# A two-layer decoder trunk: other places for modulation sums, a vector moved to the second mixing, and rotary tables on GpSimd

## The chip, the cores and the metric

The kernel runs on 1 core of a Trainium2 chip. The metric is the device time of one execution in microseconds (us). The profile names five engines: PE (matrix products), DVE (VectorE), ACT (ScalarE), POOL (GpSimd) and SP (here only a queue of DMA transfers). Each executes its own instructions in a fixed order and waits where an input is not ready.

## The reference, cut to what matters

One sequence of 256 tokens with 1024 features passes two layers, in float32. Each layer has three sub-layers: a SwiGLU feed-forward (inner width 2816), a token mixing, and a second feed-forward. Each sub-layer normalises its input and changes it by a shift, a scale and a gate that come from a vector `c`:

```python
cos, sin = rope_tables(positions, ATT_HEAD_DIM // ROPE_FRACTION)
c_act = jax.nn.silu(c)
for l in range(DEPTH):
    mod = c_act @ ada_w[l] + ada_b[l]            # 1024 x 9216
    sh1, sc1, g1, sh2, sc2, g2, sh3, sc3, g3 = jnp.split(mod, N_MOD, axis=-1)
    h = modulate(rms_norm(x, norm_ffn1[l]), sh1, sc1)
    x = x + 0.5 * g1[:, None, :] * swiglu(h, ffn1_w_in[l], ffn1_w_out[l])
    h = modulate(rms_norm(x, norm_mix[l]), sh2, sc2)
    x = x + g2[:, None, :] * token_mix(h, cos, sin, mix_w_in[l], sgu_w[l], sgu_b[l], mix_w_out[l])
    h = modulate(rms_norm(x, norm_ffn2[l]), sh3, sc3)
    x = x + 0.5 * g3[:, None, :] * swiglu(h, ffn2_w_in[l], ffn2_w_out[l])
return rms_norm(x, final_norm)
```

`modulate(h, shift, scale)` is `h * (1 + scale) + shift`. `swiglu` is `(silu(g) * u) @ w_out` with `g, u` the two halves of `h @ w_in`. `token_mix` runs a causal gating and an attention over selected keys side by side; its queries and keys are rotated by the `cos` and `sin` tables, which are computed once from the positions.

## The kernel before, in words

**Weights.** Every matrix is streamed once, in units of 512 KB. SP's queue loads a unit into one of seven raw buffers (`dma_fill`, L328; the DMAs are issued in L350 to L364). A product in full precision is made of three products of rounded parts (`mm3`, L514; L694 for both token blocks at once): high by high, high by low, low by high. So each raw unit is split before PE may use it: ACT writes the high part `whi` (L474), then DVE writes the low part `wlo` (L479), into a ring of ten pairs (`NB`). A raw buffer is free when `wlo` has been written.

**Modulation.** A vector of 1024 values takes eight more units of 512 KB, out of `ada_w`, through the same seven raw buffers and the same queue. ACT multiplies the first by a column of `c` (L454), DVE adds the other seven (L459), into `aacc`. Then the 128 partitions are still to be summed. For a shift (kind B) or a scale (kind A) `col_finish` (L397) does it with two times four PE transposes (L780) and two DVE reductions (L405). For a gate (kind G) `aacc` is itself split by L474 and L479 and multiplied by ones on PE (L374, L375; `ada_finish`, L368), and DVE adds the bias (L376). Either sum is put off by `ADA_D` = 8 work items (`defer`): it comes into the engines' queues eight items after the last of the vector's blocks.

**Six phases.** One to three are the first layer's feed-forward, mixing and feed-forward; four to six the second layer's. A feed-forward has 66 weight units: 44 of `w_in` and 22 of `w_out`. The units of `w_in` come in chunks of eight (one of four). From the second chunk on (`joint_chunk`, L686) both blocks of 128 tokens are multiplied together, 24 matmuls of 256 columns a unit. At a chunk's end ACT does silu out of PSUM (L716), DVE the product (L717), ACT and DVE the split (L511, L512). These four wait for PE to finish the chunk, and what stands behind them in the queues of ACT and DVE waits with them. Then `project` (L602) multiplies by `w_out`: block 0 runs seven units ahead of block 1 (`LAG`), half a unit's work each; afterwards the blocks take turns.

**The order of the stream.** `weave` (L256) puts modulation blocks evenly between weight units; `FA0`, `FA1` (phase one) and `F0`, `F1` (phases three to six) bound the stretch of units, `MA0`, `MA1` that of the mixings. `VA1`, `VA2`, `VA3`, `VB1`, `VB2` say how many vectors belong to each phase: before, these are five, one, four, five, none, and the rest (one) in the last. They are taken in turn from one list in the order of need (A, B, G of sub-layer one, then two, then three; the very first A and B are made at the start).

**How far splits run ahead.** `pump` (L427) emits splits and modulation blocks after each item. It stops where `lead` split weights lie ahead of PE (L444). `joint_gen` (L731) yields how many units of its chunk are left, and L1292 makes of it `min(8, 4 + left)`: toward the end of a chunk the lead shrinks from 8 to 5, but in the last chunk it stays 8 (`left` is 0 there).

**Rotary tables.** `rope_tables` (L154) is a generator; phase one takes two of its steps after each joint unit. Before, DVE does all of it (eight memsets, products, casts to integer and back, range reduction), and ACT the sines (L189 to L199).

Of the kernel before, what the change touches and what calls it, by code (L numbers as in the profile page):

```python
# [13 lines left out]
ALU = mybir.AluOpType  # L14
# [14 lines left out]
TAIL = 3  # L29
VX = 188  # L30
ADA_D = 8
D_EVP = 0
D_V = 0
D_V2 = 0
# [14 lines left out]
RED_ACT = 1  # L49
SCOL = 3  # L50
SPUMP = 0
FA0 = 20
FA1 = 62
NSRAW = 8
NV = 2
GAP = 0
VA1 = 5
VA2 = 1
VA3 = 4
VB1 = 5  # L60
VB2 = 0
F0 = 14
F1 = 62
ADA0_ACT = 1
# [31 lines left out]
PI_IN = 3.1415925  # L96
# [3 lines left out]
def trunk(ctx, tc, x_in, c_in, pos_in, ada_w, ada_b, norm_ffn1, ffn1_w_in, ffn1_w_out,  # L100
# [53 lines left out]
    def rope_tables():  # L154
        posf = small.tile([P, 2], F32, name="posf", tag="posf")
        V.tensor_copy(posf, posi)
        yield
        invt = small.tile([P, 8], F32, name="invt", tag="invt")
        for i, f in enumerate(INV_FREQ):
            V.memset(invt[:, i:i + 1], f)  # L160
            yield
        for b in range(2):
            V.tensor_scalar(ang[:, b, :], invt, posf[:, b:b + 1], None, op0=ALU.mult)
            yield
        nf = const.tile([P, 2, 8], F32, name="nf")
        ni = const.tile([P, 2, 8], I32, name="ni")
        t2 = const.tile([P, 2, 8], F32, name="t2")
        for m in (2048.0, 1.0):
            V.tensor_scalar(nf, ang, 1.0 / (2 * math.pi * m), None, op0=ALU.mult)
            yield  # L170
            V.tensor_copy(ni, nf)
            yield
            V.tensor_copy(nf, ni)
            yield
            for cc in (C1, C2, C3):
                V.scalar_tensor_tensor(ang, nf, -cc * m, ang, op0=ALU.mult, op1=ALU.add)
                yield
        V.tensor_scalar(nf, ang, math.pi, None, op0=ALU.is_gt)
        yield
        V.tensor_scalar(t2, ang, -math.pi, None, op0=ALU.is_lt)  # L180
        yield
        V.tensor_tensor(nf, nf, t2, op=ALU.subtract)
        yield
        for cc in (C1, C2, C3):
            V.scalar_tensor_tensor(ang, nf, -cc, ang, op0=ALU.mult, op1=ALU.add)
            yield
        V.tensor_scalar(ang, ang, PI_IN, -PI_IN, op0=ALU.min, op1=ALU.max)
        yield
        S.activation(sinT[:, :, 8:16], ang, AF.Sin)  # L189
        yield  # L190
        S.activation(sinT[:, :, 0:8], ang, AF.Sin, scale=-1.0)
        yield
        V.scalar_tensor_tensor(t2, ang, -1.0, ang, op0=ALU.mult, op1=ALU.max)
        yield
        V.tensor_scalar(t2, t2, -1.0, math.pi / 2, op0=ALU.mult, op1=ALU.add)
        yield
        S.activation(cosT[:, :, 0:8], t2, AF.Sin)
        yield
        S.activation(cosT[:, :, 8:16], t2, AF.Sin)  # L199
        yield  # L200
# [80 lines left out]
    for l in range(DEPTH):  # L281
        u1, chunks = ffn_units(ffn1_w_in[l], ffn1_w_out[l])
        u2 = mix_units(mix_w_in[l], mix_w_out[l])
        u3, _ = ffn_units(ffn2_w_in[l], ffn2_w_out[l])
        n_f = KD + KF
        phases += [("f", l, 1, n_f if l else KF), ("m", l, 2, len(u2)), ("f", l, 3, n_f)]
        vl = []
        for q in range(3):
            vl.append(sum((vecs(a, [nm]) for a, nm in names[:cuts[3 * l + q]]), []))
            names = names[cuts[3 * l + q]:]  # L290
        w1 = weave(u1, vl[0], FA0 if l == 0 else F0, FA1 if l == 0 else F1)
        if l == 0:
            w0 = []
            for g in range(NG):
                w0 += [dict(k="s", g=g, j0=j0) for j0 in (list(range(0, KD, SJ)) if g else
                                                     list(range(SJ, KD, SJ)) + [0])]
                w0 += [w1[2 * g], w1[2 * g + 1], w1[KD + g]]
            w1 = w0 + w1[KD + NG:]
        seq += w1
        seq += weave(u2, vl[1], MA0, MA1)  # L300
        seq += weave(u3, vl[2], F0, F1)
# [125 lines left out]
    def pump(quota=2, force=False, now=False, hi_only=False):  # L427
# [5 lines left out]
        while sp[0] < len(seq) and quota > 0:  # L433
# [15 lines left out]
            if e["k"] == "a":  # L449
                j = e["j"]  # L450
                if j == 0:
                    aacc = accs[0] = aap.tile([P, D], F32, name="aacc", tag="aacc")
                    if ADA0_ACT:
                        S.activation(aacc, e["raw"], AF.Copy, scale=ccol[:, 0:1])  # L454
                    else:
                        V.tensor_scalar(aacc, e["raw"], ccol[:, 0:1], None, op0=ALU.mult)
                else:
                    aacc = accs[0]
                    V.scalar_tensor_tensor(aacc, e["raw"], ccol[:, j:j + 1], aacc,  # L459
                                           op0=ALU.mult, op1=ALU.add)  # L460
                if j == KD - 1 and e["kind"] != "G":
                    defer(ADA_D, col_finish(e, aacc))
            if need:
                ring.append(False)
                hi = hlp.tile([P, D], F32R, name="whi", tag="whi")
# [265 lines left out]
    def joint_gen(env, first):  # L731
        for ch in range(first, len(chunks)):
            left = 8 if chunks[ch][1] == 512 else 4
            for _ in joint_chunk(env, ch):
                left -= 1
                yield left if ch + 1 < len(chunks) else 0


    def rope(t, nh, b, pool):
# [594 lines left out]
```

## Time and profile before

| what | before |
|---|---|
| time of three runs | 1011.24, 1011.47, 1011.87 us; median 1011.47 us |
| profiled execution | 1015.82 us, of which the profiled span is 1014.1 us |
| PE / DVE / ACT / POOL busy | 97% / 77% / 53% / 3% of the span |
| moved by DMA | 253.41 MB, 250 GB/s over the span |
| phase one's products by `w_out` begin | near 152.7 us |
| first, second mixing (from one norm's statistics to the next) | 220.08 to 326.77 us, 710.75 to 813.68 us |

The share of busy time is a mean over the phases. A matmul's start is exact and its end modelled, so PE's true pace is read from start to start. "PEclk" in the windows is the granted clock: 1.00 is the upper of two levels (2.4 GHz), 0.5 the lower (1.2 GHz), and numbers between are means over a stretch.

### The profile page before, as it was taken

To read this page: it belongs to the slowest core of one execution; us is meant where nothing else is said; L and a number is where in the kernel's file an instruction comes from. 1 tells how busy PE (TensorE), PEld (TensorE's weight loads), DVE (VectorE), ACT (ScalarE), POOL (GpSimd) and SP (SyncE) were. 2 spreads that over 40 slices of the span, in tenths; PEclk is the share of its full clock that TensorE was granted. 3 is DMA by queue.
4 is the path that set the end of the run, shared out by engine and by line. 5 is a ranking of instruction groups with operands and counts; after the bars stand their busy time and mean duration, and the time that the engine had idled before them with its cause. 6 is when DMAs were issued, how large, how long until landed. Compare 5 with 4: busy or idle time off the path is not lost.

```text
span 1014.1 us, 16715 instructions
## 1 busy us (share of the span) xinstructions
PE 986.3 (97%) x6468; PEld 881.0 (87%) x6468; DVE 777.9 (77%) x1088; ACT 536.3 (53%) x804; POOL 26.4 (3%) x39
## 2 busy tenths in 40 slices
PE   7999997999999999999999999999999999999997
PEld 6899995887787899998888999878778889999886
DVE  6888988777897877789678688895878785576554
ACT  6465454356577744545455454543657765454341
POOL 4000000000000000000000000000000000000000
PEclk9999998999999999999999999989999999999999
DMA  9988899956655577889858779987554556576731
GB/s 333 380 286 321 316 352 353 356 181 225 188 189 157 169 270 280 300 314 356 289 162 315 276 291 344 358 328 235 167 152 138 166 158 207 169 252 243 262 115 42
DMA packets 110031, 253.41 MB, mean 250 GB/s; under 512 B 8754, under 2 KB 27236, under 8 KB 109952
## 3 DMA queue, kind: packets, MB, share of 16 engines
q1 hardware_dynamic: 109120, 251.20, 70.8%
q8 instruction: 50, 0.82, 0.3%
q0 software_dynamic: 544, 0.63, 0.3%
q10 hardware_dynamic: 288, 0.52, 0.1%
q14 instruction: 29, 0.24, 0.1%
HBM read 251.27 MB, written 1.05 MB: 249 GB/s over the span
## 4 chain that ended last, share of the span: by engine, by line
PE 73%; DVE 12%; DMA 7%; ACT 5%; issue 3%; POOL 0%; SPq 0%; POOLq 0%; ACTq 0%; DVEq 0%
PE bank L694 28%; PE bank L515 14%; PE bank L517 13%; PE bank L516 13%; DVE wlo L479 3%; DVE aacc L459 3%; PE bank L780 2%; DMA raw<-in_ffn_w_in_dram 2%; DMA raw<-in_ffn_w_out_dram 2%; DMA sraw<-in_ada_w_dram 2%; ACT whi L474 2%; DVE xm L717 1%; ACT aThi L511 1%; DMA raw<-in_ada_w_dram 1%; DVE aacc L1101 1%
## 5 line engine op out<-in xcount | busy, mean ns | idle before, releaser
L474 ACT ACTIVATE whi<-raw 128x1024 fp32r<-128x1024 f32 (+1 forms) x328 | 334.9, 1046 | 233.1 <-PE bank L517 126.6
L479 DVE TENSOR_TENSOR wlo<-raw,whi 128x1024 fp32r<-128x1024 f32 (+1 forms) x313 | 373.9, 1212 | 91.7 <-ACT whi L474 89.7
L694 PE MATMUL bank<-hThi,whi 128*128 128x256 f32 x1216 | 336.1, 280 | 1.6 <-ACT hThi L1139 1.6
L694 PE MATMUL bank<-hThi,wlo 128*128 128x256 f32 x1216 | 333.2, 277 | 0.0
L694 PE MATMUL bank<-hTlo,whi 128*128 128x256 f32 x1216 | 323.7, 277 | 0.0
L694 PEld LDWEIGHTS bank<-hThi,whi 128*128 128x128 f32 x1216 | 228.3, 188 | 2.9 <-ACT hThi L1139 2.0
L694 PEld LDWEIGHTS bank<-hThi,wlo 128*128 128x128 f32 x1216 | 229.1, 188 | 0.7 <-issue 0.7
L694 PEld LDWEIGHTS bank<-hTlo,whi 128*128 128x128 f32 x1216 | 222.6, 188 | 0.3
L515 PE MATMUL bank<-whi,aThi 128*128 128x512 f32 (+1 forms) x374 | 144.1, 385 | 1.4 <-ACT whi L474 1.3
L516 PE MATMUL bank<-wlo,aThi 128*128 128x512 f32 (+1 forms) x374 | 143.2, 383 | 2.3 <-DVE wlo L479 2.3
L459 DVE SCALAR_TENSOR_TENSOR aacc<-raw,ccol,aacc 128x1024 f32<-128x1024 f32 x112 | 143.5, 1281 | 1.2 <-DMA raw<-in_ada_w_dram 1.2
L517 PE MATMUL bank<-whi,aTlo 128*128 128x512 f32 (+1 forms) x374 | 142.7, 381 | 0.0
L515 PE MATMUL bank<-whi,hThi 128*128 128x512 f32 (+1 forms) x352 | 140.9, 400 | 0.7 <-ACT hThi L560 0.7
L517 PE MATMUL bank<-whi,hTlo 128*128 128x512 f32 (+1 forms) x352 | 136.2, 387 | 0.0
L516 PE MATMUL bank<-wlo,hThi 128*128 128x512 f32 (+1 forms) x352 | 135.1, 384 | 0.0
L516 PEld LDWEIGHTS bank<-wlo,aThi 128*128 128x128 f32 x374 | 71.4, 191 | 16.1 <-DVE wlo L479 3.3
L515 PEld LDWEIGHTS bank<-whi,aThi 128*128 128x128 f32 x374 | 71.5, 191 | 15.3 <-ACT whi L474 1.8
L517 PEld LDWEIGHTS bank<-whi,aTlo 128*128 128x128 f32 x374 | 71.3, 191 | 13.5
L515 PEld LDWEIGHTS bank<-whi,hThi 128*128 128x128 f32 x352 | 66.2, 188 | 16.9 <-issue 2.0
L517 PEld LDWEIGHTS bank<-whi,hTlo 128*128 128x128 f32 x352 | 66.1, 188 | 14.9 <-DVE hTlo L561 0.9
L516 PEld LDWEIGHTS bank<-wlo,hThi 128*128 128x128 f32 x352 | 66.3, 188 | 11.6
L717 DVE TENSOR_TENSOR xm<-xm,bank 128x256 f32<-128x256 f32 x76 | 29.5, 416 | 54.5 <-ACT xm L716 54.4
(158 smaller groups left out, 692.5 us busy)
## 6 DMA issues: line engine op xcount, KB each, us to landing
raw<-in_ffn_w_in_dram SPq DMA_DIRECT2D x160, 512.0 KB, 5.7
raw<-in_ada_w_dram SPq DMA_DIRECT2D x128, 512.0 KB, 5.8
raw<-in_ffn_w_out_dram SPq DMA_DIRECT2D x88, 512.0 KB, 6.3
raw<-in_mix_w_in_dram SPq DMA_DIRECT2D x40, 512.0 KB, 4.4
sraw<-in_ada_w_dram SPq DMA_DIRECT2D x32, 256.0 KB, 6.1
raw<-in_ffn_w_in_dram SPq DMA_DIRECT2D x32, 256.0 KB, 3.5
raw<-in_mix_w_out_dram SPq DMA_DIRECT2D x16, 512.0 KB, 3.7
vec<-in_ada_b_dram SPq DMA_DIRECT2D x6, 512.0 KB, 7.5
```

Of the source, the lines that this page charges most:

```text
L459: V.scalar_tensor_tensor(aacc, e["raw"], ccol[:, j:j + 1], aacc, op0=ALU.mult, op1=ALU.add)
L474: S.activation(hi[:, :n], src, AF.Copy)
L479: V.tensor_tensor(lo[:, :n], src, hi[:, :n].bitcast(F32), op=ALU.subtract)
L511: S.activation(hi, ps, AF.Copy)
L515: T.matmul(ps, ahi, whi, start=first, stop=False)
L516: T.matmul(ps, ahi, wlo, start=False, stop=False)
L517: T.matmul(ps, alo, whi, start=False, stop=last)
L694: T.matmul(o, wk[stat][col], mov[:, :, k, :], start=first and i_ == 0 and mov is hThi and stat == 0, stop=False, skip_group_check=True)
L717: V.tensor_tensor(a, a, acc[j][:, 256:], op=ALU.mult)
L780: T.transpose(ps[:, i * P:(i + 1) * P], src(i), ident)
L1101: V.scalar_tensor_tensor(acc, su[g][j], ccol[:, j:j + 1], su["dps"] if j == PEJ else acc, op0=ALU.mult, op1=ALU.add)
```

## The change: what it does

- `ADA_DL` = 22: `col_finish` of the last vector of the first and the third sub-layer's list (where that is a shift or a scale) is put off by 22 items instead of 8. It concerns the scale A3 in phase one and the scale A3 in phase four.
- Phase one's 40 modulation blocks are spread over units 18 to 66 instead of 20 to 62.
- `VB1` 5 to 4 and `VB2` 0 to 1: the shift B3 of the second layer goes from phase four to the second mixing, so phase four has 32 blocks instead of 40, over the same 48 units.
- `joint_gen` yields the number of units left only where it starts at chunk two, which is phase one; in phases three, four and six the lead stays 8.
- The rotary tables' memsets and arithmetic go from DVE to GpSimd; a fused multiply-add becomes two instructions. The casts and the absolute value stay on DVE.

```diff
 ADA_D = 8
+ADA_DL = 22
-FA0 = 20
-FA1 = 62
+FA0 = 18
+FA1 = 66
-VB1 = 5
-VB2 = 0
+VB1 = 4
+VB2 = 1
...
         for i, f in enumerate(INV_FREQ):
-            V.memset(invt[:, i:i + 1], f)
+            G.memset(invt[:, i:i + 1], f)
             yield
         for b in range(2):
-            V.tensor_scalar(ang[:, b, :], invt, posf[:, b:b + 1], None, op0=ALU.mult)
+            G.tensor_scalar(ang[:, b, :], invt, posf[:, b:b + 1], None, op0=ALU.mult)
...
-            V.tensor_scalar(nf, ang, 1.0 / (2 * math.pi * m), None, op0=ALU.mult)
+            G.tensor_scalar(nf, ang, 1.0 / (2 * math.pi * m), None, op0=ALU.mult)
...
             for cc in (C1, C2, C3):
-                V.scalar_tensor_tensor(ang, nf, -cc * m, ang, op0=ALU.mult, op1=ALU.add)
+                G.tensor_scalar(t2, nf, -cc * m, None, op0=ALU.mult)
+                G.tensor_tensor(ang, ang, t2, op=ALU.add)
                 yield
...
             vl.append(sum((vecs(a, [nm]) for a, nm in names[:cuts[3 * l + q]]), []))
+            if vl[q]:
+                vl[q][-1]["last"] = q != 1
...
-                    defer(ADA_D, col_finish(e, aacc))
+                    defer(ADA_DL if e.get("last") else ADA_D, col_finish(e, aacc))
...
-                yield left if ch + 1 < len(chunks) else 0
+                yield left if first == 2 and ch + 1 < len(chunks) else 0
```

The next two pieces are DVE's order in phase one, from just behind the product and split of the last joint chunk. `wlo<-raw` is a weight's split, `aacc<-raw` a modulation block, `wlo<-aacc` the split of the gate G2, and `cs<-bank` a reduction. First the kernel before:

```order
L479 TENSOR_TENSOR wlo<-raw,whi 128x1024
L459 SCALAR_TENSOR_TENSOR aacc<-raw,ccol,aacc 128x1024
L479 TENSOR_TENSOR wlo<-aacc,whi 128x1024
L479 TENSOR_TENSOR wlo<-raw,whi 128x1024
L405 TENSOR_REDUCE cs<-bank_80 128x4
L405 TENSOR_REDUCE cs<-bank_81 128x4
L395 TENSOR_TENSOR ab<-cs,cols 128x8
L376 TENSOR_TENSOR vec<-bank_83,vec 128x512
L376 TENSOR_TENSOR vec<-bank_79,vec 128x512
```

And the changed kernel at the same place (its line numbers are five higher here):

```order
L484 TENSOR_TENSOR wlo<-raw,whi 128x1024
L464 SCALAR_TENSOR_TENSOR aacc<-raw,ccol,aacc 128x1024
L484 TENSOR_TENSOR wlo<-raw,whi 128x1024 x2
L410 TENSOR_REDUCE cs<-bank_80 128x4
L464 SCALAR_TENSOR_TENSOR aacc<-raw,ccol,aacc 128x1024
L410 TENSOR_REDUCE cs<-bank_81 128x4
L400 TENSOR_TENSOR ab<-cs,cols 128x8
L484 TENSOR_TENSOR wlo<-raw,whi 128x1024
L464 SCALAR_TENSOR_TENSOR aacc<-raw,ccol,aacc 128x1024
L484 TENSOR_TENSOR wlo<-aacc,whi 128x1024
L484 TENSOR_TENSOR wlo<-raw,whi 128x1024 x2
```

The gate's split stood behind one weight and one block; now it stands behind four weights and three blocks. On PE the four multiplications by ones that need it (L374, L375) have moved as well: they stood behind block 1's first unit of `w_out`, and stand behind its sixth now. Between the last chunk's product and the one before it, DVE had eleven weights and ten blocks, and has eleven and eight now.

ACT's order around the last joint chunk of phase four, before (`xm_107<-bank` is silu, `aThi` the split):

```order
L454 ACTIVATE aacc<-raw,ccol 128x1024
L474 ACTIVATE whi<-raw 128x1024 x8
L716 ACTIVATE xm_107<-bank_84 128x256
L716 ACTIVATE xm_107<-bank_85 128x256
L511 ACTIVATE aThi<-xm_107 128x512
L716 ACTIVATE xm_107<-bank_80 128x256
L716 ACTIVATE xm_107<-bank_83 128x256
L511 ACTIVATE aThi<-xm_107 128x512
L474 ACTIVATE whi<-raw 128x1024 x2
L454 ACTIVATE aacc<-raw,ccol 128x1024
L474 ACTIVATE whi<-raw 128x1024 x16
```

The same place in the changed kernel:

```order
L479 ACTIVATE whi<-aacc 128x1024
L479 ACTIVATE whi<-raw 128x1024 x2
L459 ACTIVATE aacc<-raw,ccol 128x1024
L479 ACTIVATE whi<-raw 128x1024
L721 ACTIVATE xm_107<-bank_81 128x256
L721 ACTIVATE xm_107<-bank_78 128x256
L516 ACTIVATE aThi<-xm_107 128x512
L721 ACTIVATE xm_107<-bank_83 128x256
L721 ACTIVATE xm_107<-bank_84 128x256
L516 ACTIVATE aThi<-xm_107 128x512
L479 ACTIVATE whi<-raw 128x1024 x17
```

The last vector that starts (L454) stood two weights behind the last silu; now the vector that is the last of the phase starts one weight ahead of it, and none starts behind.

POOL's order where the rotary work has come in (`invt`, `ang`, `nf` and `t_1028` are the tables' small tiles):

```order
L161 MEMSET invt 128x1 x8
L164 TENSOR_SCALAR ang<-invt,posf 128x8
L790 DMA xm_108<-in_sgu_w_dram 128x4x128
L791 AFFINE_SELECT xm_108<-xm_108 128x512
L164 TENSOR_SCALAR ang<-invt,posf 128x8
L170 TENSOR_SCALAR nf<-ang 128x16
L177 TENSOR_SCALAR t_1028<-nf 128x16
L178 TENSOR_TENSOR ang<-ang,t_1028 128x16
```

Of these rows only the DMA and the masking of `sgu_w` stood on POOL before; in all 35 instructions join it, eight of them memsets, and 26 leave DVE.

## Rows read from the trace of the kernel before

**Rows 1.** The page's first lines: the span, and busy time, share and instructions of each engine.

```profile
span 1014.1 us, 16715 instructions
...
PE 986.3 (97%) x6468; PEld 881.0 (87%) x6468; DVE 777.9 (77%) x1088; ACT 536.3 (53%) x804; POOL 26.4 (3%) x39
```

**Rows 2.** What PE waited for over the whole span: the waiting line and the releaser, us in total, times, longest (the rows of the start and the shorter ones left out).

```profile
PE bank L374 <- ACT whi L474: 5.9, 1, 5.9
...
PE bank L374 <- DVE xm L717: 0.9, 1, 0.9
```

**Rows 3.** Stretches of 20 us (phases one, three and four): length, busy us and instructions of PE, PEld, DVE, ACT, POOL, granted clock, DMA share, GB/s.

```profile
140.00:160.00 20.00, 20.00 (x146) 18.73 (x146) 18.18 (x19) 7.52 (x7) 0.00 (x0) 1.00 0.99 373
160.00:180.00 20.00, 12.83 (x40) 8.81 (x39) 17.14 (x22) 9.71 (x14) 0.00 (x0) 0.74 0.88 319
...
440.00:460.00 20.00, 20.00 (x178) 20.00 (x177) 18.71 (x21) 10.81 (x11) 0.00 (x0) 1.00 0.79 295
460.00:480.00 20.00, 20.00 (x100) 16.74 (x99) 18.16 (x22) 10.61 (x14) 0.00 (x0) 1.00 0.92 348
...
660.00:680.00 20.00, 18.96 (x76) 15.47 (x77) 18.30 (x19) 8.07 (x8) 0.00 (x0) 0.83 0.89 325
```

**Rows 4.** PE in order of time in phase one, as the products by `w_out` begin: start, us, line, tiles, and in brackets the idle time before and its releaser.

```profile
163.05 0.51 PE L516 MATMUL bank<-wlo,aThi 128*128 128x512 f32 x1 [0.67 <-DVE wlo L479]
...
165.84 0.40 PE L517 MATMUL bank<-whi,aTlo 128*128 128x512 f32 x1
172.17 0.79 PE L374 MATMUL bank<-whi,ones 128*128 128x512 f32 x1 [5.93 <-ACT whi L474]
...
174.87 0.63 PE L515 MATMUL bank<-whi,aThi 128*128 128x512 f32 x1
...
178.69 0.40 PE L515 MATMUL bank<-whi,aThi 128*128 128x512 f32 x1
178.93 0.39 PE L516 MATMUL bank<-wlo,aThi 128*128 128x512 f32 x1
```

**Rows 5.** DVE at the same place, in order of time.

```profile
161.78 1.22 DVE L479 TENSOR_TENSOR wlo<-raw,whi 128x1024 fp32r<-128x1024 f32 x1
162.91 1.28 DVE L459 SCALAR_TENSOR_TENSOR aacc<-raw,ccol,aacc 128x1024 f32<-128x1024 f32 x1
164.11 0.74 DVE L717 TENSOR_TENSOR xm<-xm,bank 128x256 f32<-128x256 f32 x2
...
168.54 1.23 DVE L479 TENSOR_TENSOR wlo<-raw,whi 128x1024 fp32r<-128x1024 f32 x1 [0.25 <-ACT whi L474]
169.69 1.28 DVE L459 SCALAR_TENSOR_TENSOR aacc<-raw,ccol,aacc 128x1024 f32<-128x1024 f32 x1
172.15 1.22 DVE L479 TENSOR_TENSOR wlo<-aacc,whi 128x1024 fp32r<-128x1024 f32 x1 [1.18 <-ACT whi L474]
```

**Rows 6.** PE at the same place in phase four.

```profile
658.93 0.50 PE L515 MATMUL bank<-whi,aThi 128*128 128x512 f32 x1 [1.35 <-ACT whi L474]
661.04 0.79 PE L516 MATMUL bank<-wlo,aThi 128*128 128x512 f32 x1 [1.61 <-DVE wlo L479]
...
662.05 0.63 PE L515 MATMUL bank<-whi,aThi 128*128 128x512 f32 x1
662.48 0.63 PE L516 MATMUL bank<-wlo,aThi 128*128 128x512 f32 x1
...
666.60 0.55 PE L515 MATMUL bank<-whi,aThi 128*128 128x512 f32 x1
```

**Rows 7.** SP's queue at the end of a chunk in phase four: the issue of transfers into raw buffers.

```profile
601.19 0.37 SPq L352 DMA_DIRECT2D raw<-in_ffn_w_in_dram  x1
608.12 0.34 SPq L364 DMA_DIRECT2D raw<-in_ada_w_dram  x1
```

**Rows 8.** The two mixings, from one norm's statistics to the next (columns as in rows 3).

```profile
220.08:326.77 106.69, 105.70 (x568) 84.66 (x566) 92.14 (x185) 71.01 (x137) 2.03 (x2) 1.00 0.61 190
710.75:813.68 102.93, 102.55 (x560) 83.11 (x558) 82.70 (x175) 70.04 (x136) 1.95 (x2) 1.00 0.52 156
```

**Rows 9.** Groups of PE by line and form in the first mixing (busy us, mean ns of one, idle before): the modulation's transposes.

```profile
L780 PE MATMUL bank<-ident,aacc 128*128 128x128 f32 x8 | 1.2, 272 | 0.0
```

**Rows 10.** Groups of DVE by line and form between 60 and 180 us: two of the rotary tables' groups.

```profile
L176 DVE SCALAR_TENSOR_TENSOR ang<-nf,ang 128x16 f32<-128x16 f32 x6 | 1.0, 172 | 0.1
...
L160 DVE MEMSET invt<- 128x1 f32 x8 | 0.3, 59 | 0.0
```

**Rows 11.** POOL in order of time: two powers of one column, and the masking of `sgu_w`.

```profile
220.08 0.57 POOL L538 TENSOR_TENSOR rstd<-ms,mhalf 128x1 f32<-128x1 f32 x1 [147.69 <-DVE ms L536]
230.70 1.46 POOL L538 TENSOR_TENSOR rstd<-ms,mhalf 128x1 f32<-128x1 f32 x1 [10.05 <-DVE ms L536]
...
564.54 1.30 POOL L786 TENSOR_SCALAR_AFFINE_SELECT xm<-xm 128x512 f32<-128x512 f32 x1 [2.40 <-DMA xm<-in_sgu_w_dram]
```

**Rows 12.** DVE in order of time, beside the second and the third of those.

```profile
230.53 1.22 DVE L420 TENSOR_TENSOR wlo<-raw,whi 128x1024 fp32r<-128x1024 f32 x1
...
565.26 1.66 DVE L479 TENSOR_TENSOR wlo<-raw,whi 128x1024 fp32r<-128x1024 f32 x1
```

**Rows 13.** DVE in order of time in phase one: the first cast of the second round of the rotary tables.

```profile
96.66 0.17 DVE L171 CAST ni<-nf 128x16 int32<-128x16 f32 x1
```

**Rows 14.** ACT in order of time in phase one: the first sine of the rotary tables.

```profile
111.76 0.20 ACT L189 ACTIVATE sinT<-ang 128x16 f32<-128x16 f32 x1
```

More of the change, by code (lines that the diff above doesn't have):

```diff
@@ L175, in rope_tables @@
             for cc in (C1, C2, C3):
-                V.scalar_tensor_tensor(ang, nf, -cc * m, ang, op0=ALU.mult, op1=ALU.add)
+                G.tensor_scalar(t2, nf, -cc * m, None, op0=ALU.mult)
+                G.tensor_tensor(ang, ang, t2, op=ALU.add)
                 yield
-        V.tensor_scalar(nf, ang, math.pi, None, op0=ALU.is_gt)
+        G.tensor_scalar(nf, ang, math.pi, None, op0=ALU.is_gt)
         yield
-        V.tensor_scalar(t2, ang, -math.pi, None, op0=ALU.is_lt)
+        G.tensor_scalar(t2, ang, -math.pi, None, op0=ALU.is_lt)
         yield
-        V.tensor_tensor(nf, nf, t2, op=ALU.subtract)
+        G.tensor_tensor(nf, nf, t2, op=ALU.subtract)
         yield
         for cc in (C1, C2, C3):
-            V.scalar_tensor_tensor(ang, nf, -cc, ang, op0=ALU.mult, op1=ALU.add)
+            G.tensor_scalar(t2, nf, -cc, None, op0=ALU.mult)
+            G.tensor_tensor(ang, ang, t2, op=ALU.add)
             yield
-        V.tensor_scalar(ang, ang, PI_IN, -PI_IN, op0=ALU.min, op1=ALU.max)
+        G.tensor_scalar(ang, ang, PI_IN, -PI_IN, op0=ALU.min, op1=ALU.max)
         yield
@@ L194, in rope_tables @@
         yield
-        V.tensor_scalar(t2, t2, -1.0, math.pi / 2, op0=ALU.mult, op1=ALU.add)
+        G.tensor_scalar(t2, t2, -1.0, math.pi / 2, op0=ALU.mult, op1=ALU.add)
         yield
```

## The prediction, made before the changed kernel was run

> **What bounds the kernel now.** I read the page's first lines first: PE is busy 97% of the span [rows 1], so a change can give time only where PE waits or runs at the lower clock. The waits of PE say where [rows 2]: besides the start, which the change leaves alone, one long wait of 5.9 us at a gate's multiplication by ones (L374), and 0.9 us at another gate's; three shorter ones before products by `w_out` are in [rows 4, 6]. The stretches of 20 us show the same from the other side [rows 3]: PE is full from 140 to 160 and from 440 to 480 at clock 1.00, but has 12.83 us of work at clock 0.74 from 160 to 180 (phase one), and clock 0.83 from 660 to 680 (phase four). In order of time [rows 4, 6] both holes are the same place: the joint chunks are over, block 0 runs seven units ahead at half a unit's work each, and the split weights run out.
>
> Why they run out is in DVE's order [rows 5]. The 51st weight's split starts at 161.78 and PE begins on it at 163.05, having waited 0.67. Then the last chunk's products and splits (164.11 to 168.54, 4.4 us; two waits for ACT inside) stand in the queue before the 52nd weight, which is ready at 169.77 (168.54 + 1.23); behind it come the last block of gate G2 and, after ACT, its split at 172.15. PE's next instruction is the multiplication that needs that split, so PE stands from 166.08 (the next start at the pitch of 0.24 between 178.69 and 178.93) to 172.17, and from there runs at 0.43 us from start to start until 178.69 [rows 4], nine matmuls; 0.43 is the pitch after the other wait too (662.05 to 662.48 [rows 6]). DVE itself is the late one: 18.18 of 20 us busy before [rows 3], so it has no room to catch up.
>
> **Phase one: fewer blocks by then, and the gate's sum later.** Between the last two chunks' products DVE has eight modulation blocks where it had ten, with eleven weights both times. A block costs 1.20 (162.91 to 164.11 [rows 5]): 2.4 us earlier. The rotary arithmetic leaves DVE: 18 operations of 0.172 and eight memsets of 0.059 [rows 10], 3.6 us, but most of it lies ahead of earlier waits, where DVE has some slack; I take 1.3 of it (0 to 2.5). So the 52nd weight is ready at 169.77 - 2.4 - 1.3 = 166.1 (164.9 to 167.4). PE, without the 0.9 wait [rows 2] and the 0.7 at the 51st weight [rows 4], is through with block 1's first unit at 166.1 - 0.9 - 0.7 = 164.5, and waits about 1.6 (0.4 to 2.9) there. This wait is late next; it is on the weight, no longer on the gate, whose four multiplications come five units later and take 4 x 0.23 = 0.9 at full clock. PE then reaches what it did at 178.69 before (nine matmuls after the start at 174.87) at 166.1 + 9 x 0.23 + 0.9 = 169.1, 9.6 earlier. After 1.35 and 1.61 of waiting in phase four the matmuls ran at half pace for 5.6 us, at a price of 2.6 (below) [rows 6], and a wait of 1.6 may end so too: I take off 2.6. **Gain 7.0**; bounds 0 (the weight as late as it was) and 11.2 (no wait at all: 164.5 + 2.1 + 0.9 = 167.5).
>
> DMA could hold this back. A joint unit takes 2.70 us (24 matmuls x 20 / 178, from the stretch that begins at 440 [rows 3]); with 40 blocks over 42 units 1.95 transfers of 0.524 MB go with it, 379 GB/s; over 48 units 1.83, 356 GB/s. The highest stretch moved 373 at a DMA share of 0.99 [rows 3]. So before, the demand was over what the stretch could move, and now is under it. The Trainium skill (DMA: Bandwidth & Descriptors, Specifications) gives about 358 GB/s from HBM as the limit of a core; by that the new demand would just fit and nothing late could be caught up (rival B). The 373 measured here is above that figure, so the measurement decides.
>
> **Phase four: eight blocks less, and a lead of eight.** The hole costs 1.35 and 1.61 of waiting, and half pace from 661.04 to 666.60 [rows 6]: the eleven matmuls there would take 2.6 of the 5.6 at 0.235, and four transposes 0.4 (at 0.1 each, an estimate below the modelled 1.2 for eight [rows 9]), so 2.6 are lost; together 5.6. The shift's eight blocks go, 32 stay over 48 units. Phase three has just these 32 over the same units and shows no hole (460 to 480, clock 1.00, DVE 18.16 [rows 3]). Further, with the lead at eight ACT and DVE do not stop five weights ahead at each chunk's end; before, SP's queue paused from 601.19 to 608.12 there [rows 7], as no raw buffer came free. **Gain 5.6** (4 to 6.5, if a short wait stays or small ones elsewhere go too). In phases three and six there is no hole to close: the deeper lead is worth 0 there, with 0.5 either way, since what ACT and DVE do more ahead of a silu lies beside PE's dense work.
>
> **The second mixing takes the vector.** The first mixing has eight woven blocks and takes 106.69 us, the second none and 102.93 [rows 8]. The 3.76 between them hold eight transposes for the vector, 0.8 by that estimate [rows 9], which only move from phase four and cost the same there; the other 3.0 is PE waiting for DVE, which has 92.14 us of work instead of 82.70. **Loss 3.0** (0 to 4: the difference may be another one between the layers).
>
> **The late sums.** Two times eight transposes and two reductions of a scale each go 14 items further on, into the first mixing and to the border of phases four and five. PE's work stays; DVE's reductions meet a mixing that is already late. I take **0.5** of loss (0 to 1.5).
>
> **The tables on POOL.** Thirty-five instructions join POOL, which is busy 3% [rows 1], so its own time costs nothing; what counts is who waits. ACT's sine at 111.76 needs the chain's end [rows 14], and whi splits are queued behind the sine. After the second round's two casts (the first at 96.66 [rows 13], so near 97.0) sixteen dependent operations follow. The trace has small POOL operations of 0.57 alone and 1.46 beside a `wlo` [rows 11, 12]. Half of them at the one and half at the other put the end at 97.0 + 8 x 0.57 + 8 x 1.46 = 113.2: ACT waits 1.5, or up to 4 if it comes to the sine earlier than before, and PE has at least five split weights (5 x 2.70 us) meanwhile. All at 1.46 put it at 120.4, and ACT would stand over 8 us there. I take 0 for POOL, and keep that end as a rival.
>
> **The sum.** -7.0 - 5.6 + 3.0 + 0.5 = -9.1, against a span of 1014.1 in a profiled execution of 1015.82. The runs' median, 1011.47, is 4.35 below that execution, and I take the difference off the median: 1002.4, rounded to 1002.
>
> **Rivals.** *A: slower, by the port that DVE and POOL share.* A `wlo` beside the masking took 1.66 instead of 1.22 and the POOL power 1.46 instead of 0.57 [rows 11, 12]: each slows the other. If all 27 operations other than memsets cost their neighbour on DVE 0.44, that is 11.9 us of DVE in phase one; the saved 3.6 is lost in ACT's stand of 8 us, and the 52nd weight is ready at 169.77 - 2.4 + 11.9 = 179.3 instead of 166.1. PE would be 4.4 behind the old 174.87, 0.9 for the ones behind it and some 1.5 more at half clock: +6.8, and -5.6 + 3.5 leave +4.7: 1016. It decides from a 52nd weight later than some 175. Against it: the masking covers 512 columns, the tables' operations 16, and an operation of one column took 0.57 with nothing beside it [rows 11], so what DVE loses to one should be nearer to nothing than to 0.44. The Trainium skill (SBUF — State Buffer, section on the two separate sides) says that a DVE operation with two SBUF inputs and a GpSimd operation that reads SBUF exclude each other for the whole instruction; both rows agree with it, and it speaks against this change, since both DVE streams of phase one have two such inputs.
>
> *B: phase one stays short of data.* If bytes, not DVE, set the pace (DMA share 0.99 and 1.95 transfers a unit), the 52nd weight gains only the two blocks and PE's clock still falls: gain 3 instead of 7: 1006.
>
> *C: the lead of eight puts silu late.* In phases three, four and six silu stands behind up to eight splits instead of five; three more of about 1.2 on DVE. If a chunk's banks then come free too late, 1 to 1.5 a phase: about 4 less gain: 1006. Against it: the last chunk had lead eight before already, and the next chunk takes other banks.
>
> *D: better.* No wait remains in phase one (gain 11.2) and the second mixing hides its blocks, so that only 1.0 is lost there and by the late sums: 1011.5 - 11.2 - 5.6 + 1.0 = 995.7.
>
> **Chances.** The forecast 60%, with its own range of 998.5 to 1005.5; B 17%, C 8%, D 8%, A 7%. Range 996 to 1008.5: it holds the forecast, B, C and half of D, and leaves A out. 0.2% is 2 us, about what a measurement here can tell from no change. Faster by more: forecast, B, C and D less their tails, 0.88; within it 0.06; slower 0.06, nearly all of A.
>
> **What would show it.** Right, step by step: the wait of 5.9 at the ones is gone and a wait of 1 to 4 us on `wlo` or `whi` stands before block 0's eighth unit of `w_out` in phase one; 160 to 180 has clock above 0.85; the place in phase four has no wait and clock 1.00; SP's queue no longer pauses 7 us at the chunk ends of phases three, four and six; the second mixing takes 105 to 107; POOL's small operations take 0.5 to 1.5 each and ACT waits for POOL under 4 us. Wrong: a wait of ACT for POOL of 6 us or more, `wlo` in phase one above 1.3 on the mean, the 52nd weight later than 170, or new holes at chunk ends.

## The result, and the profile after

The changed kernel takes 1001.84 us (median of four runs, 1001.32 to 1002.85), beside 1011.67 for the kernel before (1011.24 to 1012.74): ratio 0.9902, 95% interval 0.9885 to 0.992. The forecast was 1002.0. The number was right, and most of its steps; two were not, and their errors went opposite ways, so that the total came out this close is in part luck. The experiments below separate the steps.

The first lines of the page of the changed kernel; they answer to [rows 1]:

```profile
span 1001.1 us, 16720 instructions
...
PE 984.4 (98%) x6468; PEld 881.2 (88%) x6468; DVE 775.1 (77%) x1062; ACT 536.1 (54%) x804; POOL 47.5 (5%) x74
```

PE has the same 6468 instructions; 13.0 us of span have gone between the two profiled executions. By the norm's statistics (POOL's L538, now L543), which stand at the border of the phases, they went here (times in us; "again" is the kernel before, profiled a second time):

| stretch | before | again | after |
|---|---|---|---|
| start to the first mixing (phase one) | 220.08 | 221.43 | 210.48 |
| first mixing | 106.69 | 106.70 | 107.13 |
| phase three | 189.75 | 189.75 | 189.54 |
| phase four | 194.23 | 193.63 | 186.11 |
| second mixing | 102.93 | 102.91 | 107.86 |
| phase six | 186.05 | 186.05 | 186.04 |
| rest | 14.37 | 14.33 | 13.94 |

Two holes have shrunk or closed, and the second mixing has become longer. What PE waited for in the changed kernel, of the lines of `w_out` (now L520, L521); the 5.9 of [rows 2] at the gate's L374 has no successor:

```profile
PE bank L520 <- ACT whi L479: 0.9, 1, 0.9
PE bank L521 <- DVE wlo L484: 0.8, 1, 0.8
```

The stretches of 20 us that answer to [rows 3] (length, PE, PEld, DVE, ACT, POOL, clock, DMA share, GB/s):

```profile
140.00:160.00 20.00, 20.00 (x141) 18.52 (x140) 18.58 (x20) 8.79 (x10) 0.00 (x0) 1.00 1.01 394
160.00:180.00 20.00, 18.39 (x73) 14.49 (x72) 16.53 (x20) 10.66 (x13) 0.00 (x0) 0.91 0.90 322
...
640.00:660.00 20.00, 20.00 (x90) 16.55 (x89) 15.20 (x16) 8.44 (x11) 0.00 (x0) 1.00 0.77 262
660.00:680.00 20.00, 20.00 (x90) 16.57 (x89) 11.69 (x10) 7.65 (x8) 0.00 (x0) 1.00 0.88 288
```

From 160 to 180 PE has 73 matmuls instead of 40, at clock 0.91 instead of 0.74. Phase four begins 9.4 us earlier than before, so the place of its hole lies near 650 now: PE is full there at 1.00, with DVE at 15.20 and 11.69 of 20 in the two stretches, where it had 18.30. In order of time, PE in phase one (answers to [rows 4]):

```profile
163.11 0.39 PE L522 MATMUL bank<-whi,aTlo 128*128 128x512 f32 x1
164.35 0.50 PE L520 MATMUL bank<-whi,aThi 128*128 128x512 f32 x1 [0.85 <-ACT whi L479]
165.61 0.50 PE L521 MATMUL bank<-wlo,aThi 128*128 128x512 f32 x1 [0.76 <-DVE wlo L484]
...
166.64 0.63 PE L522 MATMUL bank<-whi,aTlo 128*128 128x512 f32 x1
167.06 0.63 PE L520 MATMUL bank<-whi,aThi 128*128 128x512 f32 x1
...
170.05 0.39 PE L521 MATMUL bank<-wlo,aThi 128*128 128x512 f32 x1
```

and DVE at the same place (answers to [rows 5]):

```profile
159.89 0.75 DVE L722 TENSOR_TENSOR xm<-xm,bank 128x256 f32<-128x256 f32 x2
...
164.33 1.22 DVE L484 TENSOR_TENSOR wlo<-raw,whi 128x1024 fp32r<-128x1024 f32 x1 [0.25 <-ACT whi L479]
...
175.16 1.23 DVE L484 TENSOR_TENSOR wlo<-aacc,whi 128x1024 fp32r<-128x1024 f32 x1 [1.21 <-ACT whi L479]
```

The last product begins at 159.89 instead of 164.11, the 52nd weight is ready at 165.55 (164.33 + 1.22), and PE waits for that weight, for its high part and then its low part. After the two waits the pitch falls to 0.42 between 166.64 and 167.06, the half clock, and is back by 170.05. The gate's split comes at 175.16, later than before, and nobody waits for it.

### The profile page after: what moved, and what is told of

Its sections match the earlier page's. It is cut to its first block, busy times and chain, and to the rows that moved or that the text cites. A ratio compares the mean times of both kernels' runs of the same rounds, so it can differ in the third digit from the quotient of the medians.

```text
span 1001.1 us, 16720 instructions
## 1 busy us (share of the span) xinstructions
PE 984.4 (98%) x6468; PEld 881.2 (88%) x6468; DVE 775.1 (77%) x1062; ACT 536.1 (54%) x804; POOL 47.5 (5%) x74
## 4 chain that ended last, share of the span: by engine, by line
PE 77%; DVE 11%; ACT 4%; DMA 4%; issue 3%; POOL 0%; SPq 0%; POOLq 0%; DVEq 0%; ACTq 0%
PE bank L699 33%; PE bank L520 13%; PE bank L522 13%; PE bank L521 13%; DVE wlo L484 3%; PE bank L785 2%; DVE aacc L464 2%; DMA raw<-in_ffn_w_in_dram 2%; ACT whi L479 1%; DMA sraw<-in_ada_w_dram 1%; DVE score L880 1%; DVE aacc L1106 1%; ACT sS L939 1%; DMA raw<-in_ffn_w_out_dram 1%; DVE m L879 1%
## 5 line engine op out<-in xcount | busy, mean ns | idle before, releaser
L520 PE MATMUL bank<-whi,aThi 128*128 128x512 f32 (+1 forms) x374 | 142.6, 381 | 0.9 <-ACT whi L479 0.9
L521 PE MATMUL bank<-wlo,aThi 128*128 128x512 f32 (+1 forms) x374 | 141.8, 379 | 0.8 <-DVE wlo L484 0.8
L520 PE MATMUL bank<-whi,hThi 128*128 128x512 f32 (+1 forms) x352 | 141.1, 401 | 0.6 <-ACT hThi L565 0.6
L521 PE MATMUL bank<-wlo,hThi 128*128 128x512 f32 (+1 forms) x352 | 135.1, 384 | 0.0
L520 PEld LDWEIGHTS bank<-whi,aThi 128*128 128x128 f32 x374 | 70.8, 189 | 14.2 <-ACT whi L479 1.3
L521 PEld LDWEIGHTS bank<-wlo,aThi 128*128 128x128 f32 x374 | 70.8, 189 | 13.8 <-DVE wlo L484 1.1
L520 PEld LDWEIGHTS bank<-whi,hThi 128*128 128x128 f32 x352 | 66.3, 188 | 16.4 <-issue 2.0
L521 PEld LDWEIGHTS bank<-wlo,hThi 128*128 128x128 f32 x352 | 66.3, 188 | 11.5
L721 ACT ACTIVATE xm<-bank 128x256 f32<-128x256 f32 x76 | 26.2, 378 | 62.0 <-PE bank L699 62.0
```

What stands on the lines that cost most here:

```text
L520: T.matmul(ps, ahi, whi, start=first, stop=False)
L521: T.matmul(ps, ahi, wlo, start=False, stop=False)
L721: S.activation(a, acc[j][:, :256], AF.Silu)
```

## The experiments

The theory: phase one is short of DVE work done in time, and gains by fewer blocks ahead of the last product and by the gate's later place; phase four gains by the vector that leaves it; the mixing pays for that vector on DVE; the tables are nearly free on POOL. The main rivals: the tables' room on DVE, or the bytes, decide phase one; the lead, not the vector, decides phase four.

**The kernel before, once more.** No edit.

> The kernel before, profiled a second time. The profiled execution of before took 1015.82 us, 4.3 above the median of the timed runs; that of the changed kernel 1002.85, 1.0 above its median. Theory: the holes in phase one (PE behind from 166.1 on, up to 178.7) and phase four (657 to 667) are a steady property and come again within 1 us, and the 3 us between the profiled difference (13.0) and the difference of the medians (9.8) lie in how deep the holes were in that one execution. So: span 1010 to 1014, holes of 7 to 9.4 and 4 to 6. Rival: the profiled execution is longer as a whole (all phases by the same share); then the holes are the same size and every phase is 0.1 to 0.3% shorter.

Measured: 1016.56 us in this profiled execution, span 1014.8, a little above the theory's 1014; phases as in the table above. The mixings, phases three and six repeat to 0.02, so the rival (longer as a whole) falls. The hole of phase four comes again here, but it has no fixed size: in the profiles of four kernels below in which nothing ahead of it in this phase is changed, phase four takes 190.81 (tables), 190.71 (spread), 190.50 (late sum, where some 0.8 of transposes have moved on) and 190.41 (the gate's sum). The whole stretch, first before, then the one with only the tables moved:

```profile
516.52:710.75 194.23, 191.27 (x1290) 174.95 (x1289) 156.92 (x176) 96.13 (x126) 4.04 (x4) 0.98 0.82 294
```

```profile
515.68:706.49 190.81, 188.65 (x1290) 172.98 (x1289) 156.06 (x176) 96.24 (x126) 4.01 (x5) 1.00 0.83 299
```

The clock is 0.98 in one and 1.00 in the other, with the same 1290 matmuls: it fell behind the hole in both profiled executions of the kernel before and in none of those four. The wait for the low part is 1.6 in all six; the one for the high part is 1.35 and 1.83 in the first two and 0.17 to 1.22 in the four. The runs of the kernel before go from 1010.24 to 1017.57 over all experiments; their medians beside the experiments are 1012.44 to 1012.89, beside the changed kernel 1011.67. So the theory's first half (the holes are a steady property) holds for their places, and not for their price.

**Only the spread.**

```diff
-FA0 = 20
-FA1 = 62
+FA0 = 18
+FA1 = 66
```

> The kernel before with phase one's 40 blocks over units 18 to 66 instead of 20 to 62, nothing else. Theory (the hole in phase one is blocks ahead of the last chunk's product on DVE, and a gate's sum ahead of block 0's eighth unit on PE): the 52nd weight is ready 2.4 us earlier, near 167.4, PE goes on with it instead of waiting for the gate, and 4.5 to 6.5 us of the time go: 1005 to 1007. Rival 1 (the rotary tables' room on DVE closes the hole): 2 to 3 us go, 1008.5 to 1009.5. Rival 2 (the bytes set the pace): under 2 us.

Measured: 1006.42, ratio 0.9935 (0.9923 to 0.9947). The theory's range; both rivals fall as sole causes. The 52nd weight is ready at 166.44, 3.3 earlier than before, and the waits at the place are 2.3 and 0.8, on the weight.

**Only the gate's sum later.**

```diff
-                    defer(ADA_D, ada_finish(e, hi, lo, r))
+                    defer(14 if (e["l"], e["v"]) == (0, 5) else ADA_D, ada_finish(e, hi, lo, r))
```

> The kernel before with the sum of gate G2 put off 14 items instead of 8, nothing else: the blocks stay where they were, but PE meets the multiplications by ones some units later, as in the changed kernel. Theory (the gate's place on PE is a part of phase one's gain of its own): the 52nd weight is still ready at 169.5 to 171.5, and PE begins block 0's eighth unit right there instead of near 175; 2.5 to 4.5 us go, 1008 to 1010.3. Rival (only the two blocks fewer ahead of the last product count): under 1 us, 1011.5 to 1013.

Measured: 1008.77, ratio 0.9966 (0.9954 to 0.9978): 3.7 us. The 52nd weight is as late as ever (ready at 170.24), but PE begins there:

```profile
169.04 0.49 PE L515 MATMUL bank<-whi,aThi 128*128 128x512 f32 x1 [2.32 <-ACT whi L474]
170.29 0.80 PE L516 MATMUL bank<-wlo,aThi 128*128 128x512 f32 x1 [0.76 <-DVE wlo L479]
```

instead of standing for the gate until 172.17 and beginning the weight at 174.87 [rows 4]. So order on PE alone gives 3.7, where the spread, which also moves the gate's sum, gives 6.0: a product for which nothing was urgent stood ahead of one that was ready sooner.

**Only the tables.** The diff of `rope_tables` alone.

> The kernel before with the rotary tables' memsets and arithmetic on GpSimd, nothing else. Theory: the wait of 0.9 near 108.9 goes and the 52nd weight comes 0.5 to 2.5 earlier; the gate still stands ahead of block 0's eighth unit, so 1 to 3 us go: 1008.5 to 1010.5. Rival 1 (the tables' room is what closes the hole): 4 or more go, under 1007.5. Rival 2 (ACT standing 5.6 us for the cosine, as seen in the changed kernel, delays the high parts that follow): no gain or slower, 1011 or more.

Measured: 1010.24, ratio 0.9976 (0.9964 to 0.9987): 2.2, the theory's range. The wait of 0.9 near 108.9 [rows 2] is gone, but the 52nd weight is not earlier (170.18), against the theory, and PE still stands 6.0 at the gate. Rivals 1 and 2 fall. Of the 2.2, phase one's profile shows 0.8 (219.24 against 220.08).

**The changed kernel without the tables' move.**

> The changed kernel with the rotary tables back on DVE. Theory: the wait of 0.9 near 108.9 is back or not (the gate there stands where it stood), the 52nd weight comes 0.5 to 2.5 later than 165.55, time 1002.5 to 1005. Rival 1 (the tables' move is worth nothing once the blocks are spread): within 0.7 of 1001.8. Rival 2 (the port costs more than it gives): under 1001.

Measured: 1005.62 (ratio to before 0.9925, 0.9901 to 0.9949). By the medians that is 3.8 above the changed kernel, more than expected; but the kernel before took 1012.89 beside it and 1011.67 beside the changed kernel, and by the gains (7.3 and 9.8) the tables are worth 2.6, inside the theory's 0.7 to 3.2. Here the 52nd weight is ready at 167.39, 1.8 after the changed kernel's 165.55, the waits are 2.3 and 0.8 instead of 0.85 and 0.76, and phase one is 1.7 longer (212.19): with the gate out of the way, the weight's lateness is PE's. The size is less sure than the sign: two versions below with the changed kernel's phase one have the weight at 164.22 and 163.83.

**Only the late sum.**

```diff
+ADA_DL = 22
...
+            if vl[q]:
+                vl[q][-1]["last"] = q != 1
...
-                    defer(ADA_D, col_finish(e, aacc))
+                    defer(ADA_DL if e.get("last") else ADA_D, col_finish(e, aacc))
```

> The kernel before with the last vector's sum put off 22 items instead of 8, nothing else (A3 of the first layer in phase one; in the second layer the last vector of phase four is then still B3, so that it is B3's sum that moves). Theory: the transposes and reductions cost in the mixing what they cost before, the time stays within 0.7 of 1011.5. Rival: two reductions of 0.68 fewer in the end of a phase short of DVE are worth 1 to 2 us, 1009.5 to 1010.5.

Measured: 1012.96, ratio 1.0003 (0.9992 to 1.0013). No effect; phase one is 1.7 shorter than before in its profile and the two mixings 1.3 and 1.0 longer, of which eight transposes each, some 0.8, are work that moved.

**Only the vector.**

```diff
-VB1 = 5
-VB2 = 0
+VB1 = 4
+VB2 = 1
```

> The kernel before with the second layer's shift B3 moved from phase four to the second mixing, nothing else. The profiles so far put phase four at 194.2, 193.6, 190.8, 190.7 and 190.5 us with the same work, at 186.1 in the changed kernel; the mixing at 102.9 and 107.9. Theory (eight blocks fewer close the hole of phase four): phase four near 187 (without the last vector's transposes), the second mixing 106 to 107, so the time is the old one within 2 us: 1010 to 1013. Rival (the lead of eight closes the hole): phase four stays above 189.5, and the time is 1013 to 1016.

Measured: 1012.71, ratio 0.9995 (0.9981 to 1.0009). Phase four and the second mixing:

```profile
516.53:703.65 187.12, 187.12 (x1282) 172.28 (x1281) 147.04 (x166) 94.77 (x125) 3.94 (x5) 1.00 0.79 283
703.65:810.23 106.58, 105.57 (x568) 84.56 (x566) 92.15 (x185) 70.96 (x137) 1.95 (x3) 1.00 0.60 190
```

The hole is closed (PE full over all of phase four), and the mixing gives the gain back, as the theory says. That does not yet say that the lead would not close it too.

**Only the lead.**

```diff
-                yield left if ch + 1 < len(chunks) else 0
+                yield left if first == 2 and ch + 1 < len(chunks) else 0
```

> The kernel before with the lead staying at eight in phases three, four and six, nothing else. Theory (the vector closes the hole): phase four keeps a wait at its products by the output weights, 189 to 194; time 1010.5 to 1012.5. Rival (the lead closes it): phase four at 187 to 188 with no wait there, the mixing as before, time 1006 to 1008.5. Third way (silu comes late behind eight splits): phases three and six above 190.5 and 187, time above 1013.

Measured: 1010.45, ratio 0.997 (0.9957 to 0.9983): 2.4. The same two stretches:

```profile
516.25:704.63 188.38, 188.38 (x1290) 173.36 (x1289) 156.35 (x176) 95.88 (x126) 3.95 (x5) 1.00 0.85 303
704.63:807.57 102.94, 102.58 (x559) 83.11 (x558) 82.70 (x175) 70.02 (x136) 1.95 (x2) 1.00 0.51 156
```

All 1290 matmuls are there, with all 40 blocks, and PE is full: the lead closes the hole alone. The time is above the rival's 1006 to 1008.5: in the four profiles where the clock did not fall behind the hole, phase four is 2.0 to 2.4 above 188.38, and the median run gains that much, not the 5.3 to 5.9 against the profiled executions of the kernel before. The mechanism is the rival's. Phases three and six are unchanged (189.54 and 186.05), so the third way falls.

**The changed kernel without the vector's move.** `VB1`, `VB2` back to 5 and 0.

> The changed kernel without the vector's move: B3 back in phase four, 40 blocks there with the lead at eight, none in the second mixing. Theory (the vector closes the hole): phase four 189 to 194, the second mixing near 103 or 104: 1001 to 1005, not below the changed kernel's 1001.8 by more than 1. Rival (the lead closes the hole, the vector only costs the mixing): phase four near 187.5, mixing 103 to 104, time 997 to 999.5, better than both.

Measured: 998.66 (998.36 to 1000.18), ratio to before 0.9858 (0.9832 to 0.9885). The rival is right, and this beats both kernels: its slowest run is below the changed kernel's fastest (1001.32), though the kernel before was 1.2 slower beside it. The two stretches, the one that answers to [rows 3], and PE's wait for the 52nd weight:

```profile
505.27:692.67 187.40, 187.40 (x1282) 172.58 (x1281) 154.99 (x173) 95.69 (x126) 3.95 (x5) 1.00 0.85 305
692.67:796.64 103.97, 103.53 (x568) 83.96 (x566) 84.10 (x178) 70.13 (x136) 1.95 (x2) 1.00 0.51 155
160.00:180.00 20.00, 18.93 (x82) 15.01 (x81) 17.23 (x19) 10.75 (x13) 0.00 (x0) 1.00 0.92 336
```

```profile
164.27 0.50 PE L521 MATMUL bank<-wlo,aThi 128*128 128x512 f32 x1 [0.28 <-DVE wlo L484]
```

Phase four is full with 40 blocks and the mixing costs 3.9 less than in the changed kernel. Its phase one is also 1.9 shorter (208.61): the 52nd weight is ready at 164.22, 1.3 before the changed kernel's, PE waits 0.28 for it instead of 1.61, and the clock does not fall. Half of the 1.3 is one transfer of `w_out`, for which ACT waited 1.52 near 148 in the changed kernel and 0.18 near 147 here. The edit changes nothing in phase one, so that part is put down to the execution; no repetition of either kernel's profile shows it. Phase four and the mixing alone make the vector's move 2.6 us dearer.

**The vector without its additions.** In the changed kernel, DVE's seven additions of B3 (second layer) are left out.

```diff
-                    V.scalar_tensor_tensor(aacc, e["raw"], ccol[:, j:j + 1], aacc,
-                                           op0=ALU.mult, op1=ALU.add)
+                    if (e["l"], e["v"]) != (1, 6):
+                        V.scalar_tensor_tensor(aacc, e["raw"], ccol[:, j:j + 1], aacc,
+                                               op0=ALU.mult, op1=ALU.add)
```

> The changed kernel with DVE's seven additions for the vector in the second mixing left out (its transfers, ACT's first product, transposes and reductions stay; the second layer's shift B3 is then only the first eighth of its sum). Theory (the mixing loses 3.4 us because DVE has the additions in its queue ahead of what PE waits for): the second mixing falls from 107.9 to 104 to 105, time 998 to 999.5. Rival (the vector's transfers take raw buffers and the queue from the mixing's weights): the mixing stays above 106.5, time 1001 to 1002.5.

Measured: 998.28. The second mixing, first in the changed kernel, then here:

```profile
693.26:801.12 107.86, 106.58 (x576) 85.43 (x574) 93.72 (x189) 71.07 (x137) 1.96 (x3) 1.00 0.63 188
```

```profile
690.98:796.06 105.08, 104.44 (x576) 84.71 (x574) 85.58 (x182) 71.21 (x137) 1.96 (x3) 1.00 0.61 193
```

With the transfers still there (193 GB/s) but 8.1 us less on DVE, 2.8 us of the mixing go: it is a little above the 104 to 105 expected, and below the rival's 106.5. That blocks without an addition may also free their raw buffers sooner is not told apart by this run. The rest of 1001.84 - 998.28 lies in phase one, which takes 208.23 in this profile: as in the version before, the 52nd weight comes earlier (163.83) and the clock does not fall.

**The tables' arithmetic left out.** Every engine's part of it; angles are a constant.

> The changed kernel with the rotary tables' arithmetic left out on every engine (the angles are a constant, so the rotation is wrong; the sines stay on ACT). Theory (on GpSimd it is free: what it slows on DVE and ACT's stand of 5.6 us for the cosine lie beside PE's work): within 1 us of 1001.8. Rival (the shared port and that stand still cost phase one): 998 to 1000.5, the 52nd weight 1 to 3 us before 165.5.

Measured: 1016.22, ratio 1.0035 (1.0022 to 1.0047), which neither expected. Phases three, four and six are 3.1, 3.8 and 4.5 longer than in the changed kernel, without any wait: PE's pitch is another one (last section). The run says nothing on the tables' price on POOL; what is measured is the net of the move, above.

**Without the vector, and the cosine's last operation on DVE.**

```diff
-        G.tensor_scalar(t2, t2, -1.0, math.pi / 2, op0=ALU.mult, op1=ALU.add)
+        V.tensor_scalar(t2, t2, -1.0, math.pi / 2, op0=ALU.mult, op1=ALU.add)
```

> The kernel called no_vector with the cosine's last operation (3.45 us on GpSimd, and ACT stood 5.6 us for it) on DVE again. Theory (ACT's stand is behind five or more split weights): within 0.7 of 998.7. Rival (the stand makes the high parts late in phase one): 996.5 to 997.8, the fastest so far.

Measured: 999.84 (999.33 to 1000.51), ratio 0.9875 (0.9862 to 0.9888). Not faster than 998.66, and a little outside the theory's range on the slow side; the rival falls. Its phase one took 210.53, as in the changed kernel. The fastest complete version measured is the changed kernel without the vector's move.

## Why the prediction was right, and where it was not

**Phase one: mechanism right, sum too small.** The 52nd weight was forecast at 166.1 and came at 165.55; PE was to wait 1.6 and waited 0.85 and 0.76, on the weight and not the gate, and the half clock came, as taken into account. The gain was forecast at 7.0; the profiled difference to the first mixing is 9.6, of which some 0.8 are eight transposes that moved into it. The half clock held from 166.64 to 170.05, eight matmuls, some 1.5 us and not 2.6; that and the weight's 0.55 are most of what the sum lacked. The gate's place gives 3.7 by itself; the prediction had it in the sum but spoke first of the blocks.

**The tables: sign right, size off.** 1.3 on the 52nd weight had been taken; it is nothing alone, and 1.8 with the spread, with 1.7 of phase one and 2.6 by the gains. The stand of ACT was looked for at the sine and came at the cosine, whose operation on POOL had been left out of the chain:

```profile
109.11 0.20 ACT L192 ACTIVATE sinT<-ang 128x16 f32<-128x16 f32 x1
...
118.80 0.22 ACT L200 ACTIVATE cosT<-t 128x16 f32<-128x16 f32 x1 [5.58 <-POOL t L198]
```

The chain to the sine ended at 108.58, not at 113.2. 5.58 is more than the 4 allowed for, and it cost nothing that shows: the version with that operation on DVE is no faster. The port's rival (A) needed DVE to lose 0.44 to each of 27 operations. It lost nothing: in the changed kernel the 42 weights' splits of 60 to 180 us take 1221 ns on the mean, before 1220. The price is POOL's:

```profile
103.42 1.32 POOL L182 TENSOR_SCALAR t<-ang 128x16 f32<-128x16 f32 x1
...
106.32 0.22 POOL L188 TENSOR_TENSOR ang<-ang,t 128x16 f32<-128x16 f32 x1
...
115.31 3.45 POOL L198 TENSOR_SCALAR t<-t 128x16 f32<-128x16 f32 x1 [6.74 <-DVE t L196]
```

0.22 as DVE ended a product out of PSUM and then stood still, 1.32 beside one split, and 3.45 beside three that followed each other:

```profile
115.15 1.27 DVE L464 SCALAR_TENSOR_TENSOR aacc<-raw,ccol,aacc 128x1024 f32<-128x1024 f32 x1
116.35 2.35 DVE L484 TENSOR_TENSOR wlo<-raw,whi 128x1024 fp32r<-128x1024 f32 x2
```

POOL's operation ends at 118.76, just behind these. The Trainium skill (SBUF — State Buffer, section on the two separate sides) says that a DVE operation with two SBUF inputs and a GpSimd operation that reads SBUF exclude each other for the whole instruction; the trace agrees for POOL, which waited through three in a row, while DVE's mean did not move.

**Phase four: the step that failed.** "The shift's eight blocks go, 32 stay" was given as the main cause, with the lead beside it as a further help and worth 0 elsewhere. Either closes the hole alone: the vector at 187.12 (with eight transposes, some 0.8, gone from the phase), the lead at 188.38, against 190.4 to 194.2. With both, the vector's move takes 1.3 off phase four (187.40 to 186.11), of which 0.8 are those transposes, and costs the mixing 3.9. That phase three had the same 32 blocks without a hole was true and proved nothing against the lead. The 5.6 were also read from an execution in which the clock fell; in four other profiles the hole is some 3 us smaller. In the same way the 4.35 between the profiled execution and the median was taken off as if it were a fixed offset; in part it was the depth of that hole.

One sign forecast with it came only in part: SP still pauses at a chunk's end in phase four, 7.2 us here and 6.9 before [rows 7].

```profile
613.50 0.33 SPq L369 DMA_DIRECT2D raw<-in_ada_w_dram  x1
620.72 0.33 SPq L357 DMA_DIRECT2D raw<-in_ffn_w_out_dram  x1
```

The pauses are shorter, though, not gone: from issue to issue, the five longest between 550 and 660 were 7.9, 10.6, 6.9, 7.0 and 6.3 before, and with the lead alone they are 6.8, 5.6, 5.6, 5.6 and 5.4. So the lead lets transfers go on sooner, as forecast, besides giving PE up to eight split weights instead of five while they pause; which of the two closes the hole is not shown.

**The second mixing: mechanism right.** Forecast 3.0 beside the transposes; it became 4.93 longer, to 107.86, above the 105 to 107 given as a sign, which left out the late sum's transposes. Of the 4.93, sixteen transposes (the vector's, and the late sum's) take 1.50 from start to start, which leaves 3.4. The late sum, taken at 0.5, changed nothing clear of noise alone. Summed from start to start, the 24 transposes of the attention's scores take 3.97 instead of 2.29 and the products of queries and keys 4.23 instead of 3.44; they wait for DVE:

```profile
L785 PE MATMUL bank<-ident,sS 128*128 128x128 f32 x24 | 4.5, 291 | 0.6 <-DVE u L1006 0.5 <-DVE sS L953 0.2
```

**Why the total fits.** The vector's 3.4 was paid as forecast; phase four gave less in the median run than 5.6 (the lead, which closes the hole, is worth 2.4 alone), and phase one with the tables more than 7.0. That these nearly cancel is luck. Rival B (bytes) as the limit that sets the pace is against the 394 GB/s from 140 to 160 and the gain of the gate's place without any change of bytes. But 373 GB/s was not the most that a stretch could move either: the kernel before moved 408 from 150 to 160. And data still come late in places: in the changed kernel ACT waits five times for `w_out` between 145 and 156, up to 1.5, and DVE once for ACT (1.35 at 149.55). Rival C (silu late) found no lengthening in phases three and six. Rival D did not come in the profiled execution, but the version without the vector's move is near it: 0.28 of waiting for the weight, and 1.0 in the mixing.

## What to carry to other kernels

Where a hole has two possible cures, try each alone before paying for both: here the free one (a deeper lead) was enough, and the one with a price elsewhere cost some 3 us in its company. Look at what an in-order engine has been told to do next, not only at what is late: a sum that nobody needed yet, standing ahead of a product whose data came sooner, was worth 3.7 us with no work changed. And profile the kernel before more than once; a hole after which the clock may or may not fall has no single size.

## What the runs showed of the hardware that had not been expected

A wait before a product does not fix what follows. In the profiles of the same phase four, waits of 1.35 and 1.61, and of 1.83 and 1.61, were followed by half clock, and waits of 1.22 and 1.62 (the late sum alone) were not; in phase one of the changed kernel 0.85 and 0.76 were. What decides is open.

The pitch of the joint chunks' matmuls (from start to start) has two levels at full clock. In phase six, before and then without the tables' arithmetic, the second row of each is six matmuls behind the first:

```profile
860.18 0.28 PE L694 MATMUL bank<-hThi,whi 128*128 128x256 f32 x1
...
860.86 0.28 PE L694 MATMUL bank<-hThi,whi 128*128 128x256 f32 x1
```

```profile
860.02 0.28 PE L670 MATMUL bank<-hThi,whi 128*128 128x256 f32 x1
...
860.73 0.28 PE L670 MATMUL bank<-hThi,whi 128*128 128x256 f32 x1
```

That is 113 and 118 ns. Over longer stretches the means are 113.3 and 117.8, with nothing between but mixtures; a kernel changes from one to the other at a few places, and the kernel before and its repetition do so alike. The kernel without the arithmetic has the longer pitch in all joint chunks, which is where most of its 3 to 4.5 us a phase come from (2.5, 3.3 and 3.8). The matmuls are the same, and in phase one so are their data; that run differs in where small tiles lie and in what POOL, DVE and ACT do near 100 us. The level also goes with the tables: from 112 to 130 us all five profiles with their arithmetic on POOL have 117.8, and all eight with it on DVE 113.3. On some 200 matmuls of that chunk this is 0.9 us of PE's time, a price of the move that the prediction did not have; whether it lengthens phase one, where DVE is the late one, is not shown. The cause wasn't found.
